# A Fourier branch whose transform over the positions is folded a second time

## The chip, the cores and the metric

The kernel runs on one core of a Trainium2 chip. The metric is the device time of one execution in microseconds; smaller is better. TensorE multiplies, VectorE and ScalarE do the elementwise work and empty PSUM, SyncE issues most of the transfers.

## The reference, cut to what matters

The whole is one layer of an encoder: a feed-forward block, a mixer of three branches, a second feed-forward block, for 528 positions (16 learned ones and 512 given) of 1024 channels. The change touches one branch, the Fourier mixing of 512 channels in 8 groups of 64:

```python
def fourier_mix(u):
    B, L, _ = u.shape
    ug = u.astype(jnp.float32).reshape(B, L, FOURIER_GROUPS, FOURIER_GROUP_DIM)
    y = jnp.fft.fft2(ug, axes=(1, 3), norm="ortho").real
    return y.reshape(B, L, D_FOURIER).astype(u.dtype)
```

`u` is a slice of `h @ w_in`, L is 528, and the result goes on to `@ w_fourier`. The second branch that matters here is the gated DeltaNet, whose chunked form solves a triangular system per chunk; the kernel does that by substitution on VectorE while TensorE works on the Fourier branch.

## The kernel before, in words

Channels lie on the 128 partitions and positions along the free axis. Every matrix product goes through one helper (L144), so nearly all products bear that line; a projection splits its operands into a high part and a low part of a rounded type, so a "unit" of 128 output channels is 24 products for each half of 264 positions.

The Fourier branch is done in four parts, q = 0 to 3, of 128 channels (two groups of 64) each. For each part, `mixer` (L916 to L919) runs the unit, calls `fold`, and gives other work a turn:

1. **On VectorE**, `scaled` (L532) brings the unit's result out of PSUM; L1009 to L1012 fold it once: u plus its reverse (`ue`) and u minus its reverse (`uo`), 265 positions each. The tile is `t`.
2. **Channel products** on TensorE: for the cosine (i=0) and the sine (i=1) part, three products turn 128, 128 and 9 positions into rows of PSUM; each is a matrix load of the positions and a pass of 128 columns of a constant. They are true fp32 products, each of which the trace shows as two records. ScalarE copies them to `zfold` (L1021 for the two full pieces, L1022 for the nine rows).
3. **Position products**: `zfold` against the table `tabz`, 266 output positions wide, contraction over 128, 128 and 9 positions, summed in PSUM; first the sine part (`po`), then the cosine part (`pe`).
4. ScalarE copies `po` (L1030), VectorE forms difference and sum (L1032, L1034), and L235 and L236 split the result.

Steps 2 and 3 are not written where they run. `fold` hands a generator to `side`, and `tick` (L204) resumes it when a modelled TensorE clock, `T.at`, has moved on far enough: 8 modelled us (`FW`) before the channel products and 4 (`FV`) before the position products. `drain_to("fold")` (L920) runs out those that are left after the fourth part. The DeltaNet core is such a generator too, so its place among the projection's products depends on the same modelled clock. Tile pools and a scheduler order each engine's instructions from that.

The names in the rows: `pb` and `pd` are PSUM tiles, `wh` and `wl` the high and low part of a weight, `ws` its staging buffer, `EZ`, `sub`, `tmp` the operands of the substitution loop (L1340 and L1342, VectorE), `Ad` and `Rf` its transposed blocks, read by small 32x32 products of TensorE when the loop is over.

Of the kernel before, what the change touches and what calls it, by code (L numbers as in the profile page):

```python
# [12 lines left out]
ALU = mybir.AluOpType  # L13
# [3 lines left out]
P = 128  # L17
NM = 16
S = 512
L = S + NM  # L20
# [36 lines left out]


NFOLD = L // 2 + 1
NTAB = 266  # L60


_C = {}
# [9 lines left out]
def constants():  # L73
    c = np.zeros((P, NCONST), np.float32)

    def put(n, a):
        o, w = _C[n]
        c[:, o:o + w] = a

    i = np.arange(P)  # L80
    same = (i[:, None] // 64) == (i[None, :] // 64)
    put("triF", same & (i[:, None] <= i[None, :]))
    put("triB", same & (i[:, None] >= i[None, :]))
    put("bones", same)
    put("sel0", (i[:, None] < 64) & np.ones((1, P), bool))
    put("sel1", (i[:, None] >= 64) & np.ones((1, P), bool))
    q = np.arange(64)
    put("i64", (i[:, None] % 64) == q[None, :])
    put("mF", np.where((i[:, None] % 64) <= q[None, :], 0.0, -1e30))
    put("mB", np.where((i[:, None] % 64) >= q[None, :], 0.0, -1e30))  # L90
    put("mrow", (i < NM)[:, None])
    put("epsc", np.full((P, 1), EPS))
    ang = 2 * np.pi * (np.outer(q, q) % 64) / 64
    sc = 1.0 / math.sqrt(L * 64)
    for n, f in (("c64", np.cos(ang)), ("s64", np.sin(ang))):
        b = np.zeros((P, P))
        b[:64, :64] = f * sc
        b[64:, 64:] = f * sc
        put(n, b)
    n = np.arange(3 * P)  # L100
    k = np.arange(NTAB)
    a2 = 2 * np.pi * (np.outer(n, k) % L) / L
    live = (n < NFOLD)[:, None]
    tab = np.stack([np.cos(a2) * live, np.sin(a2) * live]).reshape(2, 3, P, NTAB)
    return c, np.ascontiguousarray(tab.transpose(2, 0, 1, 3), dtype=np.float32)


class Cols:
# [42 lines left out]
class K:  # L151
# [705 lines left out]
    def mixer(self, pre, hT):  # L857
        nc, A = self.nc, self.A
# [1 line left out]
        self.x = x  # L860
        self.keep = self.t(self.dr, "keep", [P, KD, S])
        nc.sync.dma_start(self.keep, hT[:, :, NM:])
        self.tab = self.t(self.mp, "tabz", [P, 2, 3, NTAB])
        nc.sync.dma_start(self.tab, A["tab"])
        partial = self.htile()[:, :, :S]
        self.beta = None
# [5 lines left out]
        o = self.unit(A["wab"], x, ALLC)  # L872
# [43 lines left out]
        for q in range(4):  # L916
            o = self.unit(A["win"][q], x, ALLC)
# [4 lines left out]
        for q in range(4):  # L922
            o = self.unit(A["win"][28 + q], x, REAL)
# [27 lines left out]
        for m in range(KD - NT):  # L951
            o = self.outs(CS)
            w = self.load(A["wout"][m])
# [46 lines left out]
    def fold(self, q, o, fh, fl):  # L1000
        nc = self.nc
        H = L // 2
        rows = (P, P, NFOLD - 2 * P)
        u = self.t3()
        self.scaled(u, o)
        eo = self.t3()
        ue, uo = eo[:, :NFOLD], eo[:, NFOLD:2 * NFOLD]
        rev = u[:, L - 1:H:-1]
        nc.vector.tensor_tensor(ue[:, 1:H], u[:, 1:H], rev, op=ALU.add)  # L1009
        nc.vector.tensor_tensor(uo[:, 1:H], u[:, 1:H], rev, op=ALU.subtract)  # L1010
        nc.vector.tensor_copy(ue[:, 0:H + 1:H], u[:, 0:H + 1:H])
        nc.vector.memset(uo[:, 0:H + 1:H], 0.0)  # L1012

        def fold():
            z = self.t(self.mp, "zfold", [P, 2, 3, P])
            for i, (src, tb) in enumerate(((ue, "c64"), (uo, "s64"))):
                pz = self.dnp()
                for a in range(3):
                    self.T.matmul(pz[:rows[a], a * P:(a + 1) * P], src[:, a * P:a * P + rows[a]],
                                     self.c(tb), start=True, stop=True)  # L1020
                nc.scalar.copy(z[:, i, 0:2], pz[:, :2 * P].rearrange("p (a b) -> p a b", a=2))  # L1021
                nc.scalar.copy(z[:rows[2], i, 2], pz[:rows[2], 2 * P:3 * P])  # L1022
            yield FV
            pe, po = self.dnp(), self.dnp()
            for i, pp in ((1, po), (0, pe)):
                for a in range(3):
                    self.T.matmul(pp[:, :NTAB], z[:rows[a], i, a], self.tab[:rows[a], i, a],
                                     start=a == 0, stop=a == 2)
            so = self.t2()
            nc.scalar.copy(so[:, :NTAB], po[:, :NTAB])  # L1030
            y = self.t2()
            nc.vector.tensor_tensor(y[:, 0:H + 1 - NM], pe[:, NM:H + 1], so[:, NM:H + 1], op=ALU.subtract)  # L1032

            nc.vector.tensor_tensor(y[:, S - 1:H - NM:-1], pe[:, 1:H], so[:, 1:H], op=ALU.add)  # L1034
            self.split(fh[:, q], fl[:, q], y)
        self.side(fold(), FW)

    def conv(self, dst, src, wi, n):
# [512 lines left out]
def prep(i):  # L1551
    i = {k: np.asarray(v) for k, v in i.items()}
    h = np.concatenate([i["meta_tokens"], i["x"][0]], 0)
    w = i["w_in"][0]
    wab = np.zeros((D, P), np.float32)
    wab[:, :16] = w[:, 4096:4112]
    const, tab = constants()
    taps = lambda a: a.T.reshape(-1, P, 3).transpose(1, 0, 2)
    hd = lambda a: np.broadcast_to(a.T.reshape(1, 8), (P, 8))
    return {  # L1560
        "xT": np.ascontiguousarray(h.T.reshape(KD, P, L).transpose(1, 0, 2)),
        "gains": np.ascontiguousarray(i["norm_gains"][0].reshape(6, KD, P).transpose(2, 0, 1)),
        "const": const, "ident": np.eye(P, dtype=np.float32), "tab": tab,
        "wi1": lay(i["ffn1_wi"][0]), "wo1": lay(i["ffn1_wo"][0]),
        "wi2": lay(i["ffn2_wi"][0]), "wo2": lay(i["ffn2_wo"][0]),
        "win": lay(w[:, :4096]), "wab": lay(wab)[0], "wg": lay(w[:, 4112:]),
        "convw": np.ascontiguousarray(np.concatenate([taps(i["sconv_w"][0]), taps(i["dn_conv_w"][0])], 1)),
        "dnpar": np.ascontiguousarray(np.concatenate(
            [hd(i["dn_A_log"][0]), hd(i["dn_dt_bias"][0]), i["dn_norm"][0][:, None]], 1)),
        "wf": lay(i["w_fourier"][0]), "wsc": lay(i["w_sconv_out"][0]), "wdn": lay(i["w_dn_out"][0]),  # L1570
        "wout": lay(i["w_out"][0]),
    }
# [23 lines left out]
```

## Time and profile before

| what | value |
|---|---|
| median of three runs | 1287.79 us (1286.96 to 1288.63) |
| the profiled execution, its own time | 1285.96 us |
| its span, first to last instruction | 1284.1 us |
| TensorE busy (matmul) | 1267.3 us, 99% of the span |
| TensorE weight loads, beside the matmuls | 1154.3 us |
| VectorE busy | 943.4 us, 73% |
| ScalarE busy | 616.8 us, 48% |
| granted TensorE clock, mean | 0.998 |

The profiled execution is a single one; 1.86 us of its time lie outside the span, and it is 1.83 us below the median of the timed runs. Busy shares are means over the whole span; the four folds lie between 648 and 685 us.

### The profile page before, as it was taken

Reading aid. Unit: us, or ns where it says so; the run is one execution under the profiler, and the core shown is the slowest. Engines: PE = TensorE matmul, PEld = TensorE weight load, DVE = VectorE, ACT = ScalarE, POOL = GpSimd, SP = SyncE. Lnnn points to the kernel's source line nnn. Section 1 sums busy time; section 2 is a strip of 40 time slices with the busy share of each in tenths; the row PEclk is TensorE's granted clock in tenths of the full one; section 3 lists DMA queues with packets and bytes.
Section 4 is the critical chain, followed back from the end, with each engine's and each line's share of the span. In section 5 each row is a group of like instructions: output and inputs, shape, how many; then the busy total and the mean of one; then the engine's idle time right before and its main releaser. Section 6 shows DMA issues by size and latency. Waiting matters only on the chain.

```text
span 1284.1 us, 22994 instructions
## 1 busy us (share of the span) xinstructions
PE 1267.3 (99%) x9095; PEld 1154.3 (90%) x9095; DVE 943.4 (73%) x1867; ACT 616.8 (48%) x1209; POOL 13.6 (1%) x28
## 2 busy tenths in 40 slices
PE   9999999999989999999999999999999999999998
PEld 9999999999989988778977777887988999999997
DVE  7978777766578779668788578654679887777654
ACT  7665444434376542443632434333557544444436
POOL 0000000000000000000000000000200000000000
PEclk9999999999999999999999999999999999999999
DMA  7243233321354222322121212235422433333213
GB/s 249 69 148 104 95 99 99 99 92 58 99 178 149 82 89 68 102 73 83 67 67 57 68 59 74 91 93 186 152 95 83 143 109 103 99 99 95 79 50 131
DMA packets 70207, 129.53 MB, mean 101 GB/s; under 512 B 15820, under 2 KB 24140, under 8 KB 70100
## 3 DMA queue, kind: packets, MB, share of 16 engines
q1 hardware_dynamic: 64244, 124.40, 29.9%
q10 hardware_dynamic: 5088, 1.57, 0.5%
q0 software_dynamic: 768, 2.10, 0.4%
q8 instruction: 71, 1.16, 0.4%
q14 instruction: 36, 0.29, 0.1%
HBM read 120.68 MB, written 7.37 MB: 100 GB/s over the span
## 4 chain that ended last, share of the span: by engine, by line
PE 88%; DVE 5%; ACT 3%; DMA 2%; issue 1%; SPq 0%; DVEq 0%; ACTq 0%
PE pb L144 54%; PE pd L144 33%; PE pd L148 1%; DVE wl L231 1%; DVE s L405 1%; ACT wh L230 1%; DVE x L412 1%; DVE acc L303 1%; DVE h L407 1%; DMA ws<-in_win 1%; DMA ws<-in_wab 1%; DMA h<-in_xT 0%; DMA ws<-in_wout 0%; ACT y L336 0%; ACT sy L331 0%
## 5 line engine op out<-in xcount | busy, mean ns | idle before, releaser
L144 PE MATMUL pb<-x,wh 128*128 128x264 f32 (+3 forms) x1584 | 354.0, 327 | 3.9 <-DVE x L412 1.9
L144 PEld LDWEIGHTS pb<-x,wh 128*128 128x128 f32 x1584 | 247.6, 189 | 33.8 <-issue 4.6
L144 PE MATMUL pb<-x,wl 128*128 128x264 f32 (+3 forms) x792 | 220.5, 323 | 0.0
L144 PE MATMUL pb<-gh,h 128*128 128x264 f32 (+2 forms) x816 | 190.7, 319 | 3.1 <-ACT pb L346 3.1
L144 PE MATMUL pd<-x,wh 128*128 128x264 f32 (+2 forms) x1040 | 192.1, 284 | 0.0
L235 ACT CAST wh<-wf 128x1024 fp32r<-128x1024 f32 x108 | 113.6, 1052 | 149.2 <-PE pd L144 120.1
L230 ACT CAST wh<-ws 128x1024 fp32r<-128x1024 f32 (+1 forms) x110 | 105.1, 956 | 166.9 <-PE pb L144 141.5
L236 DVE TENSOR_TENSOR wl<-wf,wh 128x1024 fp32r<-128x1024 f32 x108 | 131.8, 1223 | 43.2 <-ACT wh L235 42.8
L144 PEld LDWEIGHTS pd<-x,wh 128*128 128x128 f32 x1040 | 160.0, 188 | 1.7
L231 DVE TENSOR_TENSOR wl<-ws,wh 128x1024 fp32r<-128x1024 f32 (+1 forms) x110 | 121.2, 1103 | 38.5 <-ACT wh L230 38.3
L144 PEld LDWEIGHTS pb<-x,wl 128*128 128x128 f32 x792 | 134.7, 189 | 12.4 <-DVE wl L375 0.2
L144 PE MATMUL pd<-x,wl 128*128 128x264 f32 (+2 forms) x520 | 143.8, 284 | 0.0
L144 PEld LDWEIGHTS pb<-gh,h 128*128 128x128 f32 x816 | 131.5, 188 | 13.5 <-ACT pb L346 3.7
L144 PE MATMUL pb<-gl,h 128*128 128x264 f32 (+2 forms) x456 | 123.2, 313 | 0.0
L144 PEld LDWEIGHTS pd<-x,wl 128*128 128x128 f32 x520 | 96.1, 188 | 0.4
L144 PE MATMUL pd<-h,wh 128*128 128x264 f32 (+1 forms) x294 | 82.0, 282 | 0.0
L144 PEld LDWEIGHTS pb<-gl,h 128*128 128x128 f32 x456 | 77.8, 188 | 4.2
L144 PE MATMUL pd<-l,wh 128*128 128x264 f32 (+1 forms) x288 | 81.5, 283 | 0.0
L144 PE MATMUL pd<-h,wl 128*128 128x264 f32 (+1 forms) x288 | 81.5, 283 | 0.0
L689 DVE TENSOR_TENSOR y<-y,pb 128x264 f32<-128x264 f32 (+1 forms) x128 | 48.7, 420 | 30.7 <-PE pb L144 30.7
L230 ACT CAST h<-ws 128x1024 fp32r<-128x1024 f32 (+1 forms) x40 | 38.5, 967 | 60.9 <-PE pb L144 50.5
L144 PE MATMUL pb<-y,wh 128*128 128x512 f32 x192 | 61.7, 403 | 0.0
(322 smaller groups left out, 2297.2 us busy)
## 6 DMA issues: line engine op xcount, KB each, us to landing
wf<-in_wi SPq DMA_DIRECT2D x144, 256.0 KB, 2.7
ws<-in_wo SPq DMA_DIRECT2D x64, 256.0 KB, 2.9
ws<-in_win SPq DMA_DIRECT2D x32, 512.0 KB, 3.2
ws<-in_wg SPq DMA_DIRECT2D x24, 512.0 KB, 3.3
ws<-in_wi SPq DMA_DIRECT2D x13, 512.0 KB, 3.6
ws<-in_wo SPq DMA_DIRECT2D x32, 192.0 KB, 2.5
ws<-in_wout SPq DMA_DIRECT2D x8, 512.0 KB, 3.2
h<-in_xT SPq DMA_DIRECT2D x10, 264.0 KB, 5.7
```

The lines of the kernel that those rows point to most:

```text
L144: return self.e.matmul(out, lhsT, rhs, **kw)
L148: return self.e.transpose(*a)
L230: nc.scalar.copy(h[:, :n], st[:, :n])
L231: nc.vector.tensor_tensor(l[:, :n], st[:, :n], h[:, :n].bitcast(F32), op=ALU.subtract)
L235: self.nc.scalar.copy(h, src)
L236: self.nc.vector.tensor_tensor(l, src, h.bitcast(F32), op=ALU.subtract)
L303: V.tensor_tensor(acc, acc, sq, op=ALU.add)
L405: V.scalar_tensor_tensor(t, ya[0][i][:, k, :W], self.gains[:, gpost, k:k + 1], r[:, c], op0=ALU.mult, op1=ALU.mult)
L407: V.tensor_tensor(hT[:, k, c], hT[:, k, c], t, op=ALU.add)
L412: V.scalar_tensor_tensor(x[1][:, k, c], hT[:, k, c], g, x[0][:, k, c].bitcast(F32), op0=ALU.mult, op1=ALU.subtract)
L689: V.tensor_tensor(y, y, p, op=ALU.add)
```

## The change

The once-folded halves have a symmetry of their own: for even output positions the cosine half needs only its sum with its own reverse, for odd ones only the difference, and the other way round for the sine half. The changed kernel folds both halves again on VectorE and splits the table by the parity of the output position. Four VectorE instructions per part are new: an addition of 2x132, a copy of 2, a subtraction of 2x4 and one of 2x128 elements per partition (L1027 to L1030 after the change). The table falls from 128x1596 to 128x1072 numbers. The nine positions that are over after two blocks of 128 (five of one parity, four of the other) are no longer a piece of nine: the third channel product takes a full block of 128 that starts there and overlaps the others, and the table holds zeros for its other 119 rows. Thus all channel products are 128x128, one ScalarE copy of 384 columns takes the place of L1021 and L1022, and each part has eight position products of 134 columns instead of six of 266. Each writes every second column of its PSUM tile (`pp[:, (a + i) % 2:NTAB:2]`), so that the positions come out in natural order. Line numbers after the change are 9 higher up to the fold and 17 higher behind it.

```diff
 NFOLD = L // 2 + 1
-NTAB = 266
+NLEFT = 9
+NPAR = 134
+NTAB = 2 * NPAR
...
     k = np.arange(NTAB)
-    a2 = 2 * np.pi * (np.outer(n, k) % L) / L
-    live = (n < NFOLD)[:, None]
-    tab = np.stack([np.cos(a2) * live, np.sin(a2) * live]).reshape(2, 3, P, NTAB)
-    return c, np.ascontiguousarray(tab.transpose(2, 0, 1, 3), dtype=np.float32)
+    tab = np.zeros((P, 2, 2 * NTAB), np.float64)
+    for i, f in enumerate((np.cos, np.sin)):
+        t = f(2 * np.pi * (np.outer(np.arange(L // 4 + 1), k) % L) / L)
+        par = (i, 1 - i)
+        for j in range(2):
+            tab[:, i, j * NPAR:(j + 1) * NPAR] = t[:P, par[j]::2]
+        for r in range(NLEFT):
+            j = 0 if r < 5 else 1
+            tab[r, i, NTAB + j * NPAR:NTAB + (j + 1) * NPAR] = t[P + r - 5 * j, par[j]::2]
...
-        rows = (P, P, NFOLD - 2 * P)
+        cols = (0, P + NLEFT, P)
+        Q = H // 2
...
+        ab = self.t3()
+        two = lambda a: a[:, :2 * NFOLD].rearrange("p (i n) -> p i n", i=2)
+        e2, a2 = two(eo), two(ab)
+        nc.vector.tensor_tensor(a2[:, :, 0:Q], e2[:, :, 0:Q], e2[:, :, H:Q:-1], op=ALU.add)
+        nc.vector.tensor_copy(a2[:, :, Q:Q + 1], e2[:, :, Q:Q + 1])
+        nc.vector.tensor_tensor(a2[:, :, Q + 1:Q + 5], e2[:, :, P:Q], e2[:, :, H - P:Q:-1], op=ALU.subtract)
+        nc.vector.tensor_tensor(a2[:, :, Q + 5:], e2[:, :, 0:P], e2[:, :, H:H - P:-1], op=ALU.subtract)
+
         def fold():
             z = self.t(self.mp, "zfold", [P, 2, 3, P])
-            for i, (src, tb) in enumerate(((ue, "c64"), (uo, "s64"))):
+            for i, (src, tb) in enumerate(((a2[:, 0], "c64"), (a2[:, 1], "s64"))):
                 pz = self.dnp()
                 for a in range(3):
-                    self.T.matmul(pz[:rows[a], a * P:(a + 1) * P], src[:, a * P:a * P + rows[a]],
-                                     self.c(tb), start=True, stop=True)
-                nc.scalar.copy(z[:, i, 0:2], pz[:, :2 * P].rearrange("p (a b) -> p a b", a=2))
-                nc.scalar.copy(z[:rows[2], i, 2], pz[:rows[2], 2 * P:3 * P])
+                    self.T.matmul(pz[:, a * P:(a + 1) * P], src[:, cols[a]:cols[a] + P], self.c(tb), start=True, stop=True)
+                nc.scalar.copy(z[:, i], pz[:, :3 * P].rearrange("p (a b) -> p a b", a=3))
             yield FV
             pe, po = self.dnp(), self.dnp()
             for i, pp in ((1, po), (0, pe)):
-                for a in range(3):
-                    self.T.matmul(pp[:, :NTAB], z[:rows[a], i, a], self.tab[:rows[a], i, a],
-                                     start=a == 0, stop=a == 2)
+                for a in range(2):
+                    for w, o in ((a, 0), (2, NTAB)):
+                        self.T.matmul(pp[:, (a + i) % 2:NTAB:2], z[:, i, w], self.tab[:, i, o + a * NPAR:o + (a + 1) * NPAR],
+                                      start=a == 0 and w == 0, stop=a == 1 and w == 2, skip_group_check=True)
```

The modelled clock moves less in the fold, so other work moves too. Three places follow.

TensorE, the position products of part q=0 and the channel products of q=1 (`kmT` is DeltaNet work, `const` the constant). Before:

```order
L144 MATMUL pd_7733<-kmT_7253 32x32 x2
L144 MATMUL pd_7768<-tabz_4806,zfold_7682 128x266 x3
L144 MATMUL pd_7767<-tabz_4806,zfold_7682 128x266 x3
L144 MATMUL pd_7783<-const_4550,t_1005_7663 128x128 x2
L144 MATMUL pd_7783<-const_4550,t_1005_7663 9x128
L144 MATMUL pd_7789<-const_4550,t_1005_7663 128x128 x2
L144 MATMUL pd_7789<-const_4550,t_1005_7663 9x128
L144 MATMUL pb_7674<-x_4209,wh_7669 128x264
```

After:

```order
L153 MATMUL pd_7741<-kmT_7253 32x32 x2
L153 MATMUL pd_7776<-tabz_4806,zfold_7692 128x134 x4
L153 MATMUL pd_7775<-tabz_4806,zfold_7692 128x134 x4
L153 MATMUL pd_7793<-const_4550,t_1007_7673 128x128 x3
L153 MATMUL pd_7798<-const_4550,t_1007_7673 128x128 x3
L153 MATMUL pb_7684<-x_4209,wh_7679 128x264
```

The two lots of 128x266 are now two lots of four products 128x134, and the 9x128 rows are gone from the channel products.

VectorE, the folding of part q=3 among the steps of the substitution loop. Before, the last rows up to the memset that ends the fold:

```order
L532 TENSOR_TENSOR t_1041_7920<-pb_7839,rx_4211 128x264
L1340 TENSOR_TENSOR tmp_7764<-EZ_7763,sub_7761 66x192
L532 TENSOR_TENSOR t_1041_7920<-pb_7840,rx_4211 128x264
L1342 TENSOR_TENSOR EZ_7763<-EZ_7763,tmp_7764 66x8x24
L1009 TENSOR_TENSOR t_1042_7923<-t_1041_7920 128x263
L1010 TENSOR_TENSOR t_1042_7923<-t_1041_7920 128x263
L1011 COPY t_1042_7923<-t_1041_7920 128x2
L1340 TENSOR_TENSOR tmp_7764<-EZ_7763,sub_7761 66x207
L1012 MEMSET t_1042_7923 128x2
```

After, from the second loop step behind the scaling to the last new instruction:

```order
L1357 TENSOR_TENSOR tmp_7772<-EZ_7771,sub_7769 66x156
L1020 TENSOR_TENSOR t_1045_7938<-t_1044_7935 128x263
L1359 TENSOR_TENSOR EZ_7771<-EZ_7771,tmp_7772 66x6x26
L1021 COPY t_1045_7938<-t_1044_7935 128x2
L1022 MEMSET t_1045_7938 128x2
L1357 TENSOR_TENSOR tmp_7772<-EZ_7771,sub_7769 66x175
L1027 TENSOR_TENSOR t_1046_7943<-t_1045_7938 128x2x132
L1359 TENSOR_TENSOR EZ_7771<-EZ_7771,tmp_7772 66x7x25
L1028 COPY t_1046_7943<-t_1045_7938 128x2
L1029 TENSOR_TENSOR t_1046_7943<-t_1045_7938 128x2x4
L1357 TENSOR_TENSOR tmp_7772<-EZ_7771,sub_7769 66x192
L1030 TENSOR_TENSOR t_1046_7943<-t_1045_7938 128x2x128
```

The folding of q=3 now stands between the loop's steps of widths 66x135 to 66x192, where before it stood between 66x192 and 66x207, and four new rows are part of it.

TensorE, a step of DeltaNet well behind the fold (`vmb`), with the projections' products ahead of it. Before:

```order
L148 MATMUL pd_8392<-ident_80,O_6416 128x128 x4
L148 MATMUL pd_8398<-ident_80,O_6416 128x128 x4
L144 MATMUL pb_8287<-x_4209,wh_8282 128x512
L144 MATMUL pb_8287<-x_4210,wh_8282 128x512
L144 MATMUL pb_8287<-x_4209,wl_8283 128x512
L144 MATMUL pb_8287<-x_4209,wh_8282 128x512
L144 MATMUL pb_8287<-x_4210,wh_8282 128x512
L144 MATMUL pb_8287<-x_4209,wl_8283 128x512
L144 MATMUL pd_8384<-vmb_8385,km_7251 128x128 x2
L144 MATMUL pb_8427<-y_7454,wh_8422 128x512
```

After:

```order
L157 MATMUL pd_8421<-ident_80,O_6416 128x128 x4
L157 MATMUL pd_8427<-ident_80,O_6416 128x128 x4
L153 MATMUL pb_8439<-y_7454,wh_8434 128x512
L153 MATMUL pb_8439<-y_7455,wh_8434 128x512
L153 MATMUL pb_8439<-y_7454,wl_8435 128x512
L153 MATMUL pb_8439<-y_7454,wh_8434 128x512
L153 MATMUL pb_8439<-y_7455,wh_8434 128x512
L153 MATMUL pb_8439<-y_7454,wl_8435 128x512
L153 MATMUL pd_8413<-vmb_8414,km_7251 128x128 x2
L153 MATMUL pb_8439<-y_7454,wh_8434 128x512
```

Before, `vmb` closes the last products with `x`; after, those end ahead of the transposes of `O` (`ident`), and six products with `y` stand ahead of `vmb`. Seen against the projections every DeltaNet step behind the fold comes six products later. The small products of `Rf` and `Ad`, which read the loop's result, stand behind 135 products counted from the last position product, where it was 129.

## Rows read from the trace of the kernel before

**Rows 1.** The page: busy time of the engines, granted TensorE clock over 40 slices
```profile
PE 1267.3 (99%) x9095; PEld 1154.3 (90%) x9095; DVE 943.4 (73%) x1867; ACT 616.8 (48%) x1209; POOL 13.6 (1%) x28
...
PEclk9999999999999999999999999999999999999999
```

**Rows 2.** The page: the chain that ended last, by engine
```profile
PE 88%; DVE 5%; ACT 3%; DMA 2%; issue 1%; SPq 0%; DVEq 0%; ACTq 0%
```

**Rows 3.** Stretches of the four folds, PE: us, PE busy, clock, DMA share, GB/s
```profile
648.36:650.17 1.81, 1.81 (x14) 1.00 0.00 0
...
653.98:657.45 3.47, 3.47 (x15) 1.00 0.15 58
...
657.45:659.37 1.92, 1.92 (x14) 1.00 0.40 68
...
663.87:667.24 3.37, 3.37 (x15) 1.00 0.16 19
...
672.48:674.83 2.35, 1.89 (x15) 1.00 0.00 0
...
678.30:680.77 2.47, 1.99 (x13) 1.00 0.02 7
```

**Rows 4.** Timeline, PE, position products of q=0: start us, us, engine, line
```profile
654.31 0.61 PE L144 MATMUL pd<-tabz,zfold 128*128 128x266 f32 x2
...
654.53 0.61 PE L144 MATMUL pd<-tabz,zfold 128*128 128x266 f32 x2
```

**Rows 5.** Timeline, PE, channel products of q=0 and the product behind them
```profile
648.47 0.50 PE L144 MATMUL pd<-const,t 128*128 128x128 f32 x3
...
648.69 0.48 PE L144 MATMUL pd<-const,t 128*128 128x128 f32 x2
...
650.17 0.51 PE L144 MATMUL pb<-x,wh 128*128 128x264 f32 x2
...
650.77 0.28 PE L144 MATMUL pb<-x,wl 128*128 128x264 f32 x1
```

**Rows 6.** ScalarE copies from PSUM by form: busy us, mean ns, idle before
```profile
L1021 ACT COPY zfold<-pd 128x256 f32<-128x256 f32 x8 | 2.9, 365 | 2.9 <-PE pd L144 2.9
...
L1195 ACT COPY vn<-pd 128x512 f32<-128x512 f32 x1 | 0.6, 588 | 5.1 <-PE pd L148 5.1
```

**Rows 7.** Timeline, PE, first position product of q=2, with the wait before it
```profile
674.83 0.49 PE L144 MATMUL pd<-tabz,zfold 128*128 128x266 f32 x1 [0.46 <-ACT zfold L1021]
```

**Rows 8.** Timeline, VectorE, the first fold of q=3
```profile
673.89 0.43 DVE L1009 TENSOR_TENSOR t<-t 128x263 f32<-128x263 f32 x1
...
674.23 0.43 DVE L1010 TENSOR_TENSOR t<-t 128x263 f32<-128x263 f32 x1
...
674.57 0.17 DVE L1011 COPY t<-t 128x2 f32<-128x2 f32 x1
...
674.64 0.37 DVE L1340 TENSOR_TENSOR tmp<-EZ,sub 66x207 f32<-66x207 f32 x1
```

**Rows 9.** VectorE by form, 640 to 690 us: the output differences, idle before
```profile
L1032 DVE TENSOR_TENSOR t<-pd,t 128x249 f32<-128x249 f32 x4 | 1.7, 419 | 2.8 <-PE pd L144 2.8
```

**Rows 10.** Timeline, VectorE, steps of the substitution loop and q=3's scaling
```profile
672.04 0.34 DVE L1340 TENSOR_TENSOR tmp<-EZ,sub 66x175 f32<-66x175 f32 x1
...
672.41 0.34 DVE L1342 TENSOR_TENSOR EZ<-EZ,tmp 66x175 f32<-66x175 f32 x1
...
672.67 0.42 DVE L532 TENSOR_TENSOR t<-pb,rx 128x264 f32<-128x264 f32 x1
```

**Rows 11.** Step behind the fold: products ahead, last transpose, first load
```profile
684.25:714.30 30.05, 30.05 (x130) 1.00 0.26 71
...
709.96 0.26 DVE L1364 STREAM_TRANSPOSE Rf<-Ad 32x128 f32<-32x128 f32 x1
...
714.32 0.10 PEld L144 LDWEIGHTS pd<-Rf,A 32*32 32x32 f32 x1 [0.37 <-issue]
```

**Rows 12.** The table's transfer: KB, us from issue to landing
```profile
tabz<-in_tab SPq DMA_DIRECT2D x1, 798.0 KB, 5.6
```

More of the change, by code (lines that the diff above doesn't have):

```diff
@@ L99, in constants @@
         put(n, b)
-    n = np.arange(3 * P)
     k = np.arange(NTAB)
-    a2 = 2 * np.pi * (np.outer(n, k) % L) / L
-    live = (n < NFOLD)[:, None]
-    tab = np.stack([np.cos(a2) * live, np.sin(a2) * live]).reshape(2, 3, P, NTAB)
-    return c, np.ascontiguousarray(tab.transpose(2, 0, 1, 3), dtype=np.float32)
+    tab = np.zeros((P, 2, 2 * NTAB), np.float64)
[7 more added lines that the diff above has]
+            tab[r, i, NTAB + j * NPAR:NTAB + (j + 1) * NPAR] = t[P + r - 5 * j, par[j]::2]
+    return c, np.ascontiguousarray(tab, dtype=np.float32)
 class Cols:
@@ L862, in mixer @@
         nc.sync.dma_start(self.keep, hT[:, :, NM:])
-        self.tab = self.t(self.mp, "tabz", [P, 2, 3, NTAB])
+        self.tab = self.t(self.mp, "tabz", [P, 2, 2 * NTAB])
         nc.sync.dma_start(self.tab, A["tab"])
```

## The prediction

> **What bounds the kernel now.** I read the page first. TensorE is busy for 1267.3 of 1284.1 us at full granted clock throughout [rows 1], and the chain of work that ended last lies on it for 88% [rows 2]. So what is taken from TensorE's stream counts nearly whole, unless another engine is then late. Next I took the table of stretches around the four folds. A part's position products cost 3.47 us (parts 0, 2, 3; the latter two read 3.47 and 3.48) or 3.37 (part 1); the channel products cost 1.81, 1.92, 2.35 and 2.47 [rows 3]. In the stretches of parts 0 and 1 TensorE is busy throughout. In the channel stretches of parts 2 and 3 it idles 0.46 and 0.48 us: no projection is left to put between, so it waits for ScalarE's copy into `zfold` [rows 3, 7]. Then the timeline gives the pace of single records (a true fp32 product is two), and the rows of VectorE and ScalarE say what hides the rest.
>
> **Position products, every part.** Two neighbouring records of 266 columns start 0.22 us apart [rows 4]. Two steps of 128-column records take 0.22 us, so 0.11 each [rows 5]. On the line through both points, 134 columns cost 0.11 + 6 x 0.11/138 = 0.115. After the change a part has 8 products, 16 records: 1.84 us. Part 1 stands behind full-shaped products and has no exposed first load; the others stand behind other shapes or a wait and cost 0.10 more, the difference of 3.47 and 3.37. So 3.47 becomes 1.94 and 3.37 becomes 1.84: 1.53 us saved in each, **6.12** in all. In this I assume that writing every second column of PSUM costs nothing, which no row shows; the bound is below, as a rival.
>
> The trade of nine-row records for full ones is in that sum: before, 8 full records make 1.76 of the 3.37 us, and the four nine-row records the other 1.61, 0.40 each. A record with 9 rows to contract costs more than a full one here, since it also changes the shape.
>
> **Channel products.** All become 128x128: 12 records at 0.11, 1.32 us. Part 0 falls from 1.81 to 1.32, part 1 from 1.92 to 1.32: **0.49 and 0.60**. Behind a nine-wide record the following product pays too: the first record of `pb` starts at 650.17, two end 0.51 later and one lasts 0.28, so the second starts at 650.40, 0.23 behind; the three steps to 650.77 take 0.12 each [rows 5]. That 0.11 is saved behind the channel products of parts 0 and 1 and behind the position products of parts 1 and 3: **0.44**. Parts 2 and 3 end with the wait for the copy. The last of 12 records starts 11 x 0.11 = 1.21 after the first and lasts 0.28, so 1.49; then the old idle, 0.46 and 0.48, plus a longer last copy. The copy of 256 columns takes 365 ns and one of 512 takes 588 [rows 6]; 384 lie halfway, 477, 0.11 more. So 2.06 and 2.08: **0.29 and 0.39** saved.
>
> **VectorE.** The four new instructions cost it time per part: two neighbouring ones of 263 elements start 0.34 apart, a tiny one takes 0.07 until the next [rows 8]; 2 x 0.34 + 2 x 0.08 (the 4-wide one a little longer than the copy) = 0.84 us. In parts 0 to 2 it is covered: the folding is done microseconds before TensorE comes to it, and VectorE waits 2.8 us for TensorE before the four output differences [rows 9].
>
> Part 3 is different. Its unit ends when the channel products of part 2 start. That was 672.48, and ahead of it lie savings of 1.53 (part 0) + 0.49 + 0.11 + 0.60 + 0.11 + 1.53 + 0.11 = 4.48, so 668.0. VectorE starts 0.19 behind that, as before (672.67 against 672.48) [rows 3, 10], hence at 668.2, if its loop steps ahead are done by then: they follow part 1's sums, which come 4.37 us earlier but are followed by more small work. Then, by the order, come two scalings, two first folds, the 2x132 and the 2x128 (6 x 0.34), four tiny ones (4 x 0.08), and seven loop steps between. Two dependent loop steps start 0.37 apart, but 0.26 if another instruction follows [rows 10], so 7 x 0.27 = 1.9. With 0.09 until the last result lands: 668.2 + 2.04 + 0.32 + 1.9 + 0.09 = 672.55. TensorE is at part 3's channel products after 4.48 + 0.29 + 1.53 = 6.30 of savings: 678.30 - 6.30 = 672.0. It waits 0.55 and pays 0.1 for an exposed load: **-0.65**. Bounds: 0, if VectorE's instructions pack closer by 0.08 each, and -2.0, if the steps cost 0.35 and the unit's result is taken up 0.8 late behind a 1.2 us split in the queue. Queued behind the last fold there are only loop steps, which come to the next term.
>
> **DeltaNet behind the fold.** The first reader of the loop's result stood behind 129 products at 0.233 us; it started at 714.32, and its last input was written by 710.22, a slack of 4.1 [rows 11]. After, TensorE ends part 3's position products at 684.25 less the savings up to there, 8.33 (the sum below) - 0.11 - 0.65 = 7.57, so at 676.68, and 135 x 0.233 us later, less 0.11, it is there: 708.0. VectorE's loop starts 3.5 us earlier (4.37 less the 0.84 of part 2's folding, which stands ahead of it), but part 3's new 0.84 falls into it, and by the order some eight tiny root steps (`rs`, `rq`), by 0.12 about 1.0. So it ends 1.6 to 1.7 earlier, at 708.55. TensorE waits **-0.5**; bounds 0 (if the loop's steps pack closer) and -1.9 (if the loop gains only 0.3). The six products by which this step is moved back are 1.4 us of cover; without them the wait would be 1.9.
>
> **Costed at nothing.** The ScalarE copies: one of 477 ns in place of 365 and a short one, off the path in parts 0 and 1, where `pb` products stand behind. The table: 536 KB in place of 798, which took 5.6 us to land [rows 12], and is issued at the top of the mixer, ahead of all its branches. SyncE's one weight load that moves goes ahead, not behind.
>
> **Sum.** 6.12 + 0.49 + 0.60 + 0.44 + 0.29 + 0.39 = 8.33; less 0.65 and 0.5: **7.2 us**. The profiled execution took 1285.96 (span 1284.1 and 1.86 around it), so it becomes 1278.8; it lies 1.83 below the median of the runs shown, so 1287.79 - 7.2 = **1280.6 us**. A measurement of this kernel can tell about 0.2%, 2.6 us, from no change.
>
> **Rival 1: spaced output doubles a record (0.19).** Each position product writes every second PSUM column. If PSUM takes a spaced column in the time of two, a record of 134 costs 0.23, a part 16 x 0.23 + 0.1 = 3.78, 0.31 more than before. The four then lose 1.24, the channel side still gains 2.21, and both waits vanish because TensorE comes later: 1.0 us gained, 1286.8, no change that can be told. For it: no row shows such an output, and the old products are all contiguous. Against it: a 266-column fp32 record spends 0.22/266 = 0.83 ns per column, whereas the contiguous product of 512 columns spends 0.233/512 = 0.455 [rows 4, 11]. Two columns side by side then pass in 0.91 ns, so even if a spaced column needs the time of such a pair, 0.91, the fp32 record grows only from 0.115 to 0.122, 0.5 us over 64 records. That is why the forecast has the higher chance.
>
> The Trainium skill, page "Advanced Engine Details and Errata", section "PSUM Cachelines", speaks against this change: it says that PSUM has lines of 8 bytes, two fp32 values, and that any non-contiguous pattern slows matmuls down significantly. By that rule the product with a spaced output would be slow, and the time that of this rival or the next; it gives no factor, and no run here shows one.
>
> **Rival 2: spaced output costs four times (0.06).** The same place, with the opposite sign. Gain turns to nothing when 4 x (16r + 0.1 - 3.47) = 2.2, r = 0.245 us per record, and is slower by 0.2% from r = 0.286. At four times, 0.46, a part takes 7.46, 3.99 more: 16.0 - 2.2 = 13.8 us slower, 1301.6. It would take a write that stalls the stream at each column, and the records of before show no stream slower than 0.83 ns per column.
>
> **Rival 3: VectorE becomes the bound of the fold (0.13).** The saving of TensorE is there, but part 3 waits 2.0 us and DeltaNet 1.9: 8.33 - 3.9 = 4.4, or 3 us if the small chains cost twice that much again; 1283.4 to 1284.8. For it: VectorE gets 3.4 us of new work, and two queues of small instructions move between. Against it: it idles for 2.8 us before the output differences alone [rows 9], and a large part of these waits shrinks.
>
> **How the numbers follow.** The forecast has 0.60 with its own range 1279.4 (no waits) to 1282.8 (5 us gained); rival 1 0.19, rival 3 0.13, rival 2 and other losses 0.06, more than 8.4 us gained 0.02. Faster by over 0.2%: 0.60 + 0.02 + 0.12 of rival 3 = 0.74; the same: rival 1 and 0.01 of rival 3, 0.20; slower 0.06. The range reaches from 1278.6, below the sum without waits by the spread of the runs, to 1287.2, which takes in rival 1, where the doubt is.
>
> **What would show it.** In the changed profile: 64 records that read `zfold`, all with 128 rows, starting 0.115 apart (0.12 if spaced columns cost a little, 0.23 in rival 1); no form with 9 rows or 9 columns; position stretches of 1.84 to 1.94 us; channel stretches of 1.32, 1.32, 2.06, 2.08; one idle of TensorE ahead of part 3's channel products, ended by VectorE's last subtraction; at most a short idle ahead of the first `Rf` load. The prediction is wrong if the steps of the records differ from 0.115, or if TensorE idles over 1 us at either place.

## The result

The changed kernel took 1279.02 us (median of 4 runs, 1277.03 to 1280.05) against 1287.65 for the kernel before (4 runs in the same comparison); the ratio is 0.9928, with a 95% interval of 0.9914 to 0.9943. That is 8.6 us by the medians and 9.3 by the ratio, where 7.2 was forecast. The direction is as forecast, and the gain is larger.

The page of the changed kernel's profiled execution (1280.05 us), whose second line answers to the first of [rows 1]:

```profile
span 1278.2 us, 23021 instructions
...
PE 1260.2 (99%) x9111; PEld 1155.5 (90%) x9111; DVE 943.3 (74%) x1883; ACT 616.9 (48%) x1201; POOL 13.5 (1%) x28
```

TensorE has 16 records more and 7 us less to do. The stretches of the folds, in the order of [rows 3] (channel products of part 0, position products of part 0, channel and position products of part 1, channel products of parts 2 and 3), and last the stretch between the folds and `Rf`, which answers to the first of [rows 11]:

```profile
649.81:651.06 1.25, 1.25 (x14) 1.00 0.00 0
654.84:656.77 1.93, 1.93 (x19) 1.00 0.55 223
656.77:658.03 1.26, 1.26 (x14) 1.00 0.04 7
662.49:664.23 1.74, 1.74 (x19) 1.00 0.45 111
669.44:671.50 2.06, 1.50 (x14) 1.00 0.02 4
673.44:675.95 2.51, 1.76 (x14) 1.00 0.00 0
677.80:709.25 31.45, 31.45 (x138) 1.00 0.27 75
```

From the first channel product to the end of the last position product it is 649.81 to 677.80, 27.99 us, where it was 648.36 to 684.24, 35.88: **7.89 us** less. Two neighbouring position records start 0.12 apart (0.114 from eight of them in a row), on the line drawn in the prediction, although each writes every second column:

```profile
655.06 0.51 PE L153 MATMUL pd<-tabz,zfold 128*128 128x134 f32 x3
655.18 0.51 PE L153 MATMUL pd<-tabz,zfold 128*128 128x134 f32 x3
```

TensorE's waits between 640 and 720 us, in total, number and longest: two for ScalarE's copy as before, one new one for VectorE's last subtraction, none ahead of `Rf`:

```profile
PE pd L153 <- ACT zfold L1038: 1.1, 2, 0.6
PE pd L153 <- DVE t L1030: 0.2, 1, 0.2
```

The folds began 1.45 us later than before, although nothing ahead of them is changed on TensorE. Most of this arises between 366 and 374 us. The stretches there (us, busy, records, then the granted clock as a share of full; the first line is the kernel before, the others are the changed kernel):

```profile
366.00:368.00 2.00, 2.00 (x21) 1.00 0.70 233
...
366.00:368.00 2.00, 1.93 (x15) 0.84 0.48 121
368.00:370.00 2.00, 2.00 (x12) 0.50 0.36 145
370.00:372.00 2.00, 2.00 (x15) 0.80 0.02 4
```

If the shares are taken as time at half clock, the changed kernel ran at 1.2 GHz for 0.64 + 2.0 + 0.8 = 3.4 us here, behind a wait of 2.60 us for ScalarE that ended at 366.07. The profiled execution of before waited 2.57 us at the same place, until 365.68, and shows 1.00 in all these stretches. This varies from one execution to the next, whichever the kernel, and is told apart below (`old`).

### The profile page after: what moved, and what is told of

Same layout as the page of the kernel before. It is cut to its first block, busy times and chain, and to the rows that moved or that the text cites. A ratio compares the mean times of both kernels' runs of the same rounds, so it can differ in the third digit from the quotient of the medians.

```text
span 1278.2 us, 23021 instructions
## 1 busy us (share of the span) xinstructions
PE 1260.2 (99%) x9111; PEld 1155.5 (90%) x9111; DVE 943.3 (74%) x1883; ACT 616.9 (48%) x1201; POOL 13.5 (1%) x28
## 4 chain that ended last, share of the span: by engine, by line
PE 82%; DVE 10%; DMA 2%; ACT 2%; issue 2%; SPq 1%; DVEq 0%; ACTq 0%
PE pb L153 52%; PE pd L153 29%; PE pd L157 1%; DVE wl L245 1%; DMA wf<-in_wi 1%; DVE wl L240 1%; DVE s L414 1%; DVE x L421 1%; DVE acc L312 1%; DVE h L416 1%; DMA ws<-in_wab 1%; ACT wh L239 0%; DVE h L568 0%; DMA h<-in_xT 0%; DMA ws<-in_wout 0%
```

## The experiments

**The changed kernel again (`again`), unaltered.**

> The changed kernel once more, unaltered, for its size. By the profile the folds themselves give 7.9 us (35.9 us from the first channel product to the end of the last position product before, 28.0 after). Theory A, that this is all and the rest of a run's time is scatter: 1279.7 us beside 1287.6, a ratio near 0.9939. Theory B, that something outside the folds gains another 0.7 us or more: 1278.9 or less, 0.9932 or less.

Measured: 1278.61 us (6 runs) against 1288.58 (15 runs), ratio 0.9929 (0.9915 to 0.9943). The folds take 27.99 us, the same to the hundredth. A ratio of 0.9932 or less was theory B's, but its interval holds theory A's 0.9939 too. What the folds give is settled, 7.9 us; whether there is another 0.7 us outside them is not.

**Full left-over pieces without the second fold (`pad`), on the kernel before.**

```diff
-    n = np.arange(3 * P)
+    n = np.concatenate([np.arange(2 * P), np.arange(NFOLD - P, NFOLD)])
...
-    live = (n < NFOLD)[:, None]
+    live = ((np.arange(3 * P) < 2 * P) | (n >= 2 * P))[:, None]
...
-                    self.T.matmul(pz[:rows[a], a * P:(a + 1) * P], src[:, a * P:a * P + rows[a]],
+                    self.T.matmul(pz[:, a * P:(a + 1) * P], src[:, cols[a]:cols[a] + P],
...
-                    self.T.matmul(pp[:, :NTAB], z[:rows[a], i, a], self.tab[:rows[a], i, a],
+                    self.T.matmul(pp[:, :NTAB], z[:, i, a], self.tab[:, i, a],
```

> The kernel before with the left-over pieces alone made full: the third channel product takes the last 128 positions, the table has zeros in the 119 rows that overlap, one copy of 384 columns; no second fold, products still 266 wide. Theory A, that the change of shape is what the nine-row pieces cost: 12 position records of 0.2245 instead of 3.47 or 3.37 us, 0.68 saved per part, and the whole gain on the channel side, 2.2: 4.9 us less than before, 1282.7. Rival, that a record costs by its columns alone whatever its rows: nothing on the position side, at most the 9-wide channel products' share, 2 us or less, 1285.6 or more.

Measured: 1283.56 us, ratio 0.9965 (0.9952 to 0.9979), 4.5 us less than before, 5.0 by the medians. The stretches of part 0 (channel, position), of part 1's position products and of part 2's channel products:

```profile
650.58:651.83 1.25, 1.25 (x14) 1.00 0.00 0
655.62:658.42 2.80, 2.80 (x16) 1.00 0.41 162
...
664.15:666.64 2.49, 2.49 (x14) 1.00 0.27 94
671.97:674.03 2.06, 1.49 (x14) 1.00 0.00 0
```

2.80 us where it was 3.47 [rows 3], with the same number of products of the same width and 119 rows of zeros more in each third one. The folds as a whole take 30.92 us, 4.96 less than before. So of the 7.89 us that the change gains in the folds, 4.96 come without a number less being computed.

The weight loads (PEld) of the kernel before, part 0's position products, show where a visit to the nine rows costs its time:

```profile
653.98 0.75 PEld L144 LDWEIGHTS pd<-tabz,zfold 128*128 128x128 f32 x4
655.07 0.29 PEld L144 LDWEIGHTS pd<-tabz,zfold 9*128 9x128 f32 x2 [0.35 <-issue]
655.71 0.75 PEld L144 LDWEIGHTS pd<-tabz,zfold 128*128 128x128 f32 x4 [0.35 <-issue]
```

Among full records the loads follow one another without idling, each beside the record ahead of its own. At each change of shape, into the nine rows and out of them, the loads stop for 0.35 us, and the next one begins only with its own record. That the late load, and nothing else that the change of shape brings, makes these steps long fits the rows, but no run separates the two.

**The second fold with left-over pieces of nine (`nine`), on the changed kernel.**

```diff
-                    self.T.matmul(pz[:, a * P:(a + 1) * P], src[:, cols[a]:cols[a] + P], self.c(tb), start=True, stop=True)
-                nc.scalar.copy(z[:, i], pz[:, :3 * P].rearrange("p (a b) -> p a b", a=3))
+                    self.T.matmul(pz[:rows[a], a * P:(a + 1) * P], src[:, cols[a]:cols[a] + rows[a]], self.c(tb), start=True, stop=True)
+                nc.scalar.copy(z[:, i, 0:2], pz[:, :2 * P].rearrange("p (a b) -> p a b", a=2))
+                nc.scalar.copy(z[:NLEFT, i, 2], pz[:NLEFT, 2 * P:3 * P])
...
-                        self.T.matmul(pp[:, (a + i) % 2:NTAB:2], z[:, i, w], self.tab[:, i, o + a * NPAR:o + (a + 1) * NPAR],
+                        self.T.matmul(pp[:, (a + i) % 2:NTAB:2], z[:rows[w], i, w], self.tab[:rows[w], i, o + a * NPAR:o + (a + 1) * NPAR],
```

> The changed kernel with the left-over pieces as they were (nine positions in a channel product, nine rows in the contraction), the second fold kept. Theory A: each visit to a nine-row shape costs about 0.28 us over full records, there are four per part now, so a part's position products take 1.9 + 1.1 = 3.0 us against 3.47, the channel side gains nothing: 1.8 us less than before at most, less the wait of part 3: about 1286.2. Rival, that the second fold carries the gain: position products near 2.0 us, 6 us less than before, 1281.6.

Measured: 1290.81 us (10 runs, 1288.22 to 1294.72), ratio 1.0028 (1.0016 to 1.0041): slower than before. Neither theory said that. The folds take 38.57 us. Position products of parts 0 and 2, then channel and position products of part 3:

```profile
653.58:656.97 3.39, 3.39 (x19) 1.00 0.19 71
...
674.26:677.65 3.39, 3.39 (x17) 1.00 0.00 0
677.65:680.58 2.93, 2.48 (x13) 0.71 0.00 0
680.58:686.53 5.95, 5.94 (x16) 0.50 0.16 44
```

At full clock the position products take 3.39 us, hardly less than the 3.47 of twice the width: with four visits to the nine-row shape per part, the change of shape eats what the second fold saves. A visit costs (3.39 - 1.93)/4 = 0.37 us, more than the 0.28 of theory A. Then, in part 3, the clock falls to 1.2 GHz; it stays there until about 692 us, in the projections behind the fold. The last position products take 5.95 us instead of 3.39, and the stretch from the fold to `Rf` 34.22 instead of 31.45. What TensorE did before the clock fell was the whole fold of part 2 and the channel products of part 3, all with nine-row or nine-wide pieces, with a wait of 0.46 us between. The kernel before has the same parts there with fewer such visits, and its clock did not fall there in either of its two profiles; that the nine-row records made it fall is not shown. In this execution the lower clock cost 2.56 us in the last position products, some 0.46 in the channel products ahead of them (2.93 against the 2.47 of before [rows 3]) and 2.77 behind, 5.8 us together, which is more than the 3.6 by which the kernel is slower. Without it the folds would take some 35.5 us, an estimate from these rows, 0.3 less than before. So at full clock the second fold alone gains next to nothing, and it is the clock that makes the kernel slower, as far as one profiled execution tells.

**Contiguous output (`contig`).** The parities are written side by side, and VectorE reads them interleaved.

```diff
-                        self.T.matmul(pp[:, (a + i) % 2:NTAB:2], z[:, i, w], self.tab[:, i, o + a * NPAR:o + (a + 1) * NPAR],
+                        self.T.matmul(pp[:, (a + i) % 2 * NPAR:((a + i) % 2 + 1) * NPAR], z[:, i, w], self.tab[:, i, o + a * NPAR:o + (a + 1) * NPAR],
...
+            alt = lambda a: a[:, :NTAB].rearrange("p (s n) -> p n s", s=2)
```

> The changed kernel with the two parities written side by side in PSUM instead of into every second column; VectorE reads them interleaved, in three instructions instead of two per part. If spaced output costs nothing: position records start 0.114 us apart as in the changed kernel and the time is its own within 1 us (VectorE has some 0.1 us more work per part, off the path). If a spaced output costs a part of a record: records below 0.114, down to 0.107, 0.4 us less in all, or more if the rule on lines holds in a stronger form.

Measured: 1278.21 us, ratio 0.9928 (0.9914 to 0.9942), the changed kernel's own. The position products of parts 0 and 1:

```profile
654.38:656.31 1.93, 1.93 (x19) 1.00 0.56 208
...
662.02:663.81 1.79, 1.79 (x18) 1.00 0.34 94
```

1.93 with either output, 1.79 against 1.74, and the records start 0.114 us apart here too. The folds take 27.77 us, 0.22 less than the changed kernel's, because part 3's channel stretch is 2.26 us long instead of 2.51. For these fp32 products spaced output costs nothing.

**The same question at a faster pace (`bench`).** 64 products whose results nothing reads, behind the folds of the changed kernel; all else is computed as before.

```diff
         self.drain_to("fold")
+        xb = self.t(self.mp, "t2", [P, 1024], mybir.dt.bfloat16, 4)
+        nc.vector.tensor_copy(xb[:, 0:384], x[0][:, 0, 0:384])
+        for s in (1, 2):
+            bp = self.dnp()
+            for r in range(32):
+                self.T.e.matmul(bp[:, 0:256 * s:s], xb[:, 256:384], xb[:, 0:256], start=True, stop=True, skip_group_check=True)
```

> The changed kernel with 64 products more behind the folds whose results nothing reads: bf16, 128x128 by 256 columns, 32 with side-by-side output and 32 writing every second column. If spaced output costs nothing even at this pace, both sets start 0.107 to 0.117 us apart. If a spaced column takes the time of a pair, the second set starts about 0.23 us apart.

Measured in one execution, the 32 products with contiguous output and then the 32 with spaced output (us, busy, records that fall in the stretch):

```profile
681.39:684.89 3.50, 3.50 (x32) 1.00 0.02 5
684.89:691.54 6.65, 6.65 (x33) 1.00 0.00 0
```

3.50/32 = 0.109 us each, and 6.65/31 steps = 0.215: twice the time, for 256 columns 0.84 ns per spaced column against 0.43 side by side. A spaced column costs as much as a pair. The Trainium skill, page "Advanced Engine Details and Errata", section "PSUM Cachelines", says that any non-contiguous pattern slows matmuls down significantly: for these bf16 products the trace agrees, with a factor of two, and for the true fp32 products of the change `contig` shows that it does not hold. The figures give a reason: a true fp32 record needs 0.84 ns for a column anyway (0.2245 us for 266 columns, the mean step in `pad`), so the fp32 stream is just slow enough.

**VectorE's new instructions twice (`twice`).**

```diff
+        for _ in range(2):
-        nc.vector.tensor_tensor(a2[:, :, 0:Q], e2[:, :, 0:Q], e2[:, :, H:Q:-1], op=ALU.add)
+            nc.vector.tensor_tensor(a2[:, :, 0:Q], e2[:, :, 0:Q], e2[:, :, H:Q:-1], op=ALU.add)
...
```

> The changed kernel with its four new VectorE instructions issued twice (the second time they write the same numbers), 0.84 us more VectorE work per part. If VectorE's fold of part 3 ends the wait ahead of its channel products: that stretch grows from 2.52 us to about 3.4. For the step behind the fold two theories: the prediction's, that the substitution loop's end sets it, gives a wait of 0.8 to 1.7 us ahead of the first product of Rf and some 1281 us in all; the rival, that the loop has room because VectorE waits in its queue for a projection's result (L978) ahead of the transposes, gives no wait there and 1279.5 us.

Measured: 1280.15 us, ratio 0.9941 (0.9929 to 0.9953). TensorE's waits between 640 and 720 us:

```profile
PE pd L153 <- ACT zfold L1039: 1.1, 2, 0.6
PE pd L153 <- DVE t L1028: 0.9, 1, 0.9
PE pd L153 <- ACT t L1048: 0.5, 1, 0.5
PE pd L153 <- DVE t L1031: 0.4, 1, 0.4
```

(L1028 and L1031 are the first addition and the last subtraction here.) The folds take 30.18 us, 2.2 more than the changed kernel's, more than the 0.85 expected. Part 3 waits 1.3 us for VectorE, and part 0's position stretch grows by 0.74 through a wait for the copy of `po`. So VectorE's new work has some cover in the changed kernel, but not for as much again. There is no wait at `Rf`. TensorE itself comes 2.2 us later, so that alone does not tell the two theories of that step apart, but VectorE's timeline does. L978 is the instruction that takes up a projection's result ahead of the transposes, here and then in the next run, `swap`:

```profile
707.06 0.69 DVE L978 TENSOR_TENSOR t<-pb,rx 128x512 f32<-128x512 f32 x1 [2.96 <-PE pb L153]
...
703.01 0.69 DVE L978 TENSOR_TENSOR t<-pb,rx 128x512 f32<-128x512 f32 x1 [2.88 <-PE pb L153]
```

Counted from the start of the folds, the loop ends at 49.9 us in the changed kernel, at 52.6 here and at 49.8 in `swap`. The last `Rf` transpose ends at 59.45, 61.66 and 58.84, each time 0.01 us behind the start of the first `Rf` product. So the transposes move with TensorE, whose result L978 waits for, and not with the loop: the rival holds.

**The sine half first (`swap`).**

```diff
-            for i, (src, tb) in enumerate(((a2[:, 0], "c64"), (a2[:, 1], "s64"))):
+            for i, src, tb in ((1, a2[:, 1], "s64"), (0, a2[:, 0], "c64")):
```

> The changed kernel with the sine half's channel products and copy ahead of the cosine half's, as the position products begin with the sine half. The wait of 0.57 us for the second copy in parts 2 and 3 then is one for the first copy, which ends about 0.5 us earlier: 0.4 to 0.5 saved in each, 0.9 us in all, 1277.8 us. If ScalarE's queue or PSUM holds the position products back all the same: no change.

Measured: 1276.93 us, ratio 0.9916 (0.9903 to 0.993). The channel products of part 2 and the stretch of its position products behind:

```profile
667.22:668.68 1.46, 1.46 (x15) 1.00 0.02 6
668.68:670.81 2.13, 2.09 (x17) 1.00 0.00 0
```

The channel stretch falls from 2.06 to 1.46, as the position products need the sine half first; the stretch behind it grows from 1.94 to 2.13, so that part 2 gains 0.41. But TensorE then comes earlier to part 3 and waits more for VectorE (0.4 us): the folds take 27.35 us, 0.64 less, not 0.9.

**VectorE's folding at a higher priority (`early`).**

```diff
+        u, eo, ab = self.t3(), self.t3(), self.t3()
+        with self.tc.high_priority(FOLDP):
+            self.scaled(u, o)
...
```

> The changed kernel with the folding on VectorE scheduled at a higher priority, so that of the seven loop steps that stand between part 3's scaling and its last subtraction two are left. If those steps are what TensorE waits for ahead of part 3's channel products, that stretch falls from 2.52 to about 2.1 us and the time by 0.4, to 1278.4; the loop ends no later, as its steps are only moved. If the wait has another cause: no change in that stretch.

Measured: 1277.14 us, ratio 0.9918 (0.9906 to 0.9931). Part 3's channel stretch:

```profile
671.21:673.28 2.07, 1.50 (x14) 1.00 0.08 28
```

2.07 instead of 2.51, as expected. So 0.44 us is what the wait of part 3 costs in the changed kernel.

**Both (`both`).**

> The changed kernel with the sine half first and the folding at higher priority. The two gains lie at different waits, so they add: 1.3 us less than the changed kernel, 1277.4 us, and no wait of TensorE over 0.2 us in the folds.

Measured: 1279.23 us, ratio 0.9936 (0.9924 to 0.9948), no better than the changed kernel, though the folds take 26.36 us, 1.63 less, without a wait. The gain is given back at `Rf`, as the timeline shows (VectorE's split of a weight, which the scheduler here put ahead of the transposes, and TensorE's wait):

```profile
703.53 1.23 DVE L241 TENSOR_TENSOR wl<-ws,wh 128x1024 fp32r<-128x1024 f32 x1 [0.16 <-ACT wh L240]
...
707.92 0.21 PE L154 MATMUL pd<-Rf,A 32*32 32x32 f32 x1 [1.62 <-DVE Rf L1381]
```

The stretch behind it, with the clock in the third number:

```profile
709.00:712.00 3.00, 3.00 (x9) 0.58 0.02 5
```

TensorE comes 1.63 us sooner and waits 1.62; then the mean granted clock of the next 3 us is 0.58 of full. From the end of the loop (699.28) it is 8.64 us to the product that waited: two transfers, the split and the transposes lie between. Counted from the start of the folds the loop ends 1.1 us later than in the changed kernel.

**Both, with room behind (`room`).** As `both`, and the DeltaNet steps from `Rf` on nine projection products later.

```diff
-        yield 3.0
+        yield 5.0 if slack == S1 else 3.0
```

> The kernel of the run named both, with the products of Rf and the DeltaNet steps behind them put nine projection products (2.1 us) later. In that run TensorE came 1.6 us too early to Rf and the clock fell behind the wait. If that was the whole loss: no wait at Rf, full clock behind it, 1.6 us less than the changed kernel, 1277.0 to 1277.4 us beside some 1278.8. If a later step of DeltaNet is then late instead, the gain goes there: 1278.5 or more.

Measured: 1276.17 us (1273.47 to 1277.75), ratio 0.9911 (0.9896 to 0.9926): the lowest median of all, though its interval overlaps those of `swap` and `early`. No wait between 640 and 720 us, full clock there. Part 3's channel products and position products:

```profile
671.43:672.89 1.46, 1.46 (x14) 1.00 0.01 6
672.89:674.73 1.84, 1.84 (x17) 1.00 0.37 138
```

The kernel is faster than the one before. Against the changed kernel its median is 2.4 us below that of `again`, but the two intervals overlap; what is shown is 1.63 us in the folds of the traces, and no wait behind them.

**The DeltaNet steps six products earlier (`lead`), on the changed kernel.**

```diff
-        yield 3.0
+        yield 1.6 if slack == S1 else 3.0
```

> The changed kernel with the products of Rf and the DeltaNet steps behind them six projection products (1.4 us) earlier, where they stood before the change. In the changed kernel TensorE reached Rf 9.5 us after the loop's last step; two transfers and VectorE's transposes need 8.6 to 9.0 of these, by the other runs. If so: TensorE comes after 8.1 us and waits 0.5 to 0.9 us, 1279.3 us or somewhat more if the clock falls behind the wait. If the tie was none, because a projection's result in VectorE's queue moves along with TensorE: no wait, the time of the changed kernel.

Measured: 1279.84 us, ratio 0.994 (0.9927 to 0.9954). One wait ahead of `Rf`:

```profile
705.93 0.21 PE L153 MATMUL pd<-Rf,A 32*32 32x32 f32 x1 [0.68 <-DVE Rf L1381]
```

0.68 us, within the 0.5 to 0.9 expected. The second half of the group, which reads the last transpose, is held up again:

```profile
706.45 0.21 PE L153 MATMUL pd<-Rf,A 32*32 32x32 f32 x1
```

That is 59.51 us after the start of the folds, where it is 59.75 in the changed kernel. Six products are 1.38 us, and 0.24 are left of them; so the changed kernel has some 0.2 us to spare at this step, and owes it to the six products by which the step moved back. The last transpose ends at 59.45 us in both.

**The kernel before under the profiler again (`old`).**

> The kernel before, unaltered, once more under the profiler, for its granted clock. In the timed runs its mean clock was 0.998 or 0.999 in 5 of 15 (1285.8 to 1287.3 us) and 0.994 to 0.996 in 8 (1288.6 to 1290.4 us). If the fold's nine-row products leave the clock to fall in some executions, a run of the slower sort shows a stretch at half clock between 670 and 700 us; if the clock falls only behind the first feed-forward block (near 367 us), as in the changed kernel's profile, none there.

Measured: 1290.17 us, one of the longer executions, mean clock 0.994. From 366 us on:

```profile
366.00:368.00 2.00, 1.69 (x10) 0.50 0.38 102
368.00:370.00 2.00, 2.00 (x10) 0.50 0.41 164
370.00:372.00 2.00, 2.00 (x12) 0.50 0.02 4
372.00:374.00 2.00, 2.00 (x17) 0.93 0.27 61
```

The clock is at half for over 6 us; from 672 to 690 us it is full, and the folds take 35.88 us, as in the first profile. So the scatter of the runs comes in good part from this place behind the first feed-forward block, in both kernels: the folds began at 648.36 and 651.22 us in the two profiles of before, and between 646.94 and 651.36 in the twelve others, all of which show the same 5058 records on TensorE up to there. In the seven traces whose clock fell at this place they began at 648.78 to 651.36, in the seven others at 646.94 to 648.37.

## Why the forecast came out as it did

**Bound: right.** What is taken from TensorE counts nearly whole.

**Position products: right.** 1.94 and 1.84 were forecast, 1.93 and, in part 1, 1.74 measured; the 0.1 in part 1 is the saving behind the last product, which I had put under "behind". The same holds for part 3, where the stretch is 1.85 (675.95 to 677.80). The pace is 0.114 as forecast. That spaced output is free was assumed, with the right bound: a spaced column at the price of a pair (0.91 ns there, 0.84 in `bench`) and an fp32 column at 0.84 cost the same. Rivals 1 and 2 are refuted by `contig` and by the records, rival 3 by the waits: VectorE cost TensorE 0.44 us at part 3, not 2.0, and nothing at `Rf`, not 1.9.

**Channel products: right.** 1.25 and 1.26 against 1.32, the difference coming out of the 0.11 that I had booked behind each; 2.06 against 2.06 in part 2. The shape, not the work, was what cost: `pad` alone gives 4.96 us in the folds where I had worked out 4.9 from the same steps.

**The wait of part 3: mis-sized.** Forecast 0.65, measured 0.44 (2.51 in the changed kernel, 2.07 in `early`). Of this the wait itself is 0.2, where I had 0.55, and the dearer restart behind it the rest (busy 1.76 against 1.50 in `early`), where I had 0.1. VectorE's last subtraction is the cause, as forecast.

**DeltaNet: the term that failed.** I booked 0.5 us there; there is no wait, with some 0.2 us to spare (`lead`). The step that failed is that I let the loop's end set the last transpose, at the distance carried over from before. My sum put TensorE at `Rf` 59.6 us after the start of the folds (708.0 less 648.36) and the last transpose at 60.2 (708.55). In the changed kernel, whose folds start at 649.81, it is 59.44 and 59.45: the transpose is written 0.7 us sooner than forecast, at 709.26. The products that read it stand in the second half of a group whose first starts at 709.25, and the group is not held up:

```profile
705.88 0.69 DVE L978 TENSOR_TENSOR t<-pb,rx 128x512 f32<-128x512 f32 x1 [3.38 <-PE pb L153]
...
709.00 0.26 DVE L1381 STREAM_TRANSPOSE Rf<-Ad 32x128 f32<-32x128 f32 x1
```

I overlooked that VectorE idles 3.38 us ahead of L978: it is a projection's result, which TensorE itself makes, and not VectorE's load, that stands ahead of the transposes, so they come sooner as TensorE does (`twice`, `swap`). The trace of before has the same wait, ahead of the last instruction in front of its transposes:

```profile
706.78 0.69 DVE L924 TENSOR_TENSOR tabz<-pb,rx 128x512 f32<-128x512 f32 x1 [2.85 <-PE pb L144]
```

That it is nearly a tie, and that the six products are its cover, was right; `both` and `lead` show what happens once the cover is gone.

**Sum and range.** With 0.44 and 0 in place of 0.65 and 0.5 the forecast's own sum is 8.33 - 0.44 = 7.89 us, which is what the folds gained. The timed gain is 8.6 to 9.3 us. The 0.7 to 1.4 us beyond the folds were not found in a trace, and the interval (7.3 to 11.1 us) does not require them; that stays open. The traces cannot settle it: from the end of the folds to the end of the span it is 599.9 and 601.2 us in the two profiles of before, 600.4 and 599.2 in the two of the changed kernel. A gain of more than 8.4 us had a chance of 0.02 in the prediction. The lower end of my range, 1278.6, lay 0.85 us below the sum without waits, after the spread of three runs. The clock behind the first feed-forward block moves single executions by some 3 us, so a lower end by the spread of more runs had to lie further down; by the median the time is inside the range, by the ratio it is 1287.79 x 0.9928 = 1278.5, just outside.

## What to carry to other kernels

Look for small left-over pieces in a dense stream of products: here a piece of nine rows cost more than a full one, as the weight loads stopped at each change of shape, and padding it with zeros cost nothing. Two improvements of an arithmetic kind and of a shape kind need not add: here the second fold alone gained next to nothing at full clock, and on top of padding it gave another 2.9 us in the folds. Before carrying a distance between two events over from the old trace, look at what the engine waits for in between. After speeding up one stage, look at the next place where two chains meet; here the whole of a further gain went into a wait there until that step was moved back as well.

## What the runs showed of the hardware

A product with every second PSUM column as output takes twice as long in bf16 (0.215 against 0.109 us for 256 columns), and as long as a contiguous one in true fp32 (0.114 us for 134 columns). At one and the same wait of TensorE (near 363 to 366 us), the granted clock was then 1.2 GHz for none (seven traces), some 3.4 us (four) or some 6.8 us (three) in different executions of the same instructions, and how long TensorE had idled did not decide it: behind 2.76 us in `room` the clock stayed full, behind 1.31 us in `again` it was down for 3.4 us. The clock also fell in a stretch in which TensorE was busy nearly throughout, but with nine-row records and short waits among the products (`nine`, 678 to 692 us).
